# Linear attention's values as seven half-size products, with the norm's root moved behind the projections

## The chip, the cores and the metric

The kernel runs on one core of a Trainium2 chip. The metric is the device time of one execution in microseconds; the median of three runs of the kernel before is 2203.17 us (2202.41 to 2204.3). One more execution was taken by the hardware profiler, and all rows of the profile come from it.

## The reference

One layer of a hybrid encoder on 512 tokens of width 2048, in float32. What matters here is the first part:

```python
h = rms_norm(x, norm_mix_w[i])
proj = h @ w_in[i]
q_a, k_a, v_a, q_g, k_g, v_g, r_g, gate_lr = split_cols(proj, IN_SPLITS)
y_a = chunked_band_attention(q_a, k_a, v_a, att_rel_bias[i])          # 16 heads of 64
gate_logit = gate_lr @ w_gla_gate_up[i] + b_gla_gate[i]               # rank 16 -> 512
log_a = log_sigmoid(gate_logit) / GLA_GATE_TAU
o_g = gated_linear_attention(q_g, k_g, v_g, log_a)                    # 4 heads, values 256 wide
y_g = rms_norm(o_g, gla_norm_w[i]) * silu(r_g)
x = x + concat(y_a, y_g) @ w_out[i]
```

`rms_norm(x, w)` is `x * rsqrt(mean(x*x) + eps) * w`. Behind it come a gated MLP with a causal convolution (`w_ffn_up`, `w_ffn_down`), a gated per-layer embedding and a last norm; the change does not touch them.

## The kernel before, in words

**Products.** Every float32 operand is split into a rounded high half (`fp32r`, made by ScalarE with a copy) and a low half (the difference, made by VectorE), and a product of two is three matmuls: high by high, high by low, low by high. Most projections are done by Strassen's scheme in Winograd's form: a 2 x 2 block product with seven half-size products `P1` to `P7` instead of eight. Their operands are, on the weights' side, the four quarters `L11` to `L22` and the sums `S1` to `S4`, and on the input's side the quarters `R11`, `R21`, `R22` and the differences `N1`, `N2`, `T3`, `T4`. The results are collected into the quarters `C11`, `C12`, `C21`, `C22`.

**The front** has three parts, all on pages of 128 x 1024 weights (512 KB).
1. `first_values`: the first half of linear attention's values (`w_v_g`) as a plain product, eight pages (`values_page`, 24 matmuls of 512 columns each). Beside it `load_input` loads the sixteen tiles of x and splits each into the halves `h1`, weighted by `norm_mix_w`; `sq_acc` adds up the squares. At the last page `first_stats` makes the norm's root, by token (`rtok`) and spread over all partitions (`rb`), with the tiny matmuls `ms` and `pb`. `values_out` multiplies the values by `rtok`.
2. `second_values`: `gate_rank` first (`plr`, 32 matmuls on `h1`), then the other half of these values, eight pages again. Between pages VectorE and ScalarE scale x by weight and root (`scale_pair`), make the Strassen operands (`right`, `differences`, `spread_differences`) and run the forget gate (`gate_low`, `gate_up` with the matmuls `pz`, `gate_abs` to `gate_ln`). The list `todo` says at which page.
3. `values_product` for attention's values (`w_v_a`): seven products of four pages, 12 matmuls of 512 columns a page (tiles `vaA` to `vaD`). The sums `S1` to `S4` of weights are made by DMAs of the POOL queue that add in flight onto a page in SBUF (`sum_more`); two pages are summed on VectorE (`sum_right`). A page is split two pages ahead of its product (`value_split(v, n + 2)`); the dictionary `plan` says what else is done at which page.

TensorE, VectorE, ScalarE and in the third part also the SP and POOL queues follow the order in which the program writes these steps.

**After the front** the stage `in` makes, with seven products of 24 matmuls (256 columns) each, four units of keys and queries of linear attention (`linear`), eight of attention (`attend`) and four of the output gate (`after_gates`). Their input operands hold the norm's root already, so the results need no scaling. The work on a unit's result is put on an agenda, a list of (steps after the unit's end, place in the step, function). In `attend`, `low` makes the low halves of queries and, twice on different partitions, of keys (`Kl`). Then follow the output projection and the other stages, where the root `rb2` multiplies results of a projection (`after_up`, `after_gate`).

PSUM has eight banks: four for values (`psum_mm`) and four by turns for other things (`psum_aux`) in the front, and one pool of banks behind it.

Of the kernel before, what the change touches and what calls it, by code (L numbers as in the profile page):

```python
# [14 lines left out]
P = 128  # L15
T = 512
# [26 lines left out]
def encoder_block(ctx: ExitStack, tc: tile.TileContext, A, out):  # L43
# [8 lines left out]
    pctx = ExitStack()  # L52
    pm = pctx.enter_context(tc.tile_pool(name="pm", bufs=4, space=PSUM))
    pa = pctx.enter_context(tc.tile_pool(name="pa", bufs=4, space=PSUM))
# [31 lines left out]
    pw = pa.tile([P, T], F32, tag="aux", name="pw")  # L86
# [28 lines left out]
    aux = [lambda name: pa.tile([P, T], F32, tag="aux", name=name)]  # L115

    def psum_mm(name):
        return pm.tile([P, T], F32, tag="mm", name=name)

    def psum_aux(name):  # L120
        return aux[0](name)

    chores, hold = [], [1]
# [7 lines left out]
    def wtile(src, name, parts=1, between=None):  # L131
        n = src.shape[1]
        raw = page("wr", name + "_r")
        hi, lo = weight_pages()
        w = n // parts
        for i in range(parts):
            if i and between is not None:
                between()
            c = slice(i * w, (i + 1) * w)
            syn.dma_start(raw[:, c], src[:, c])  # L140
            act.activation(hi[:, c], raw[:, c], AF.Copy)
            vec.tensor_tensor(lo[:, c], raw[:, c], hi[:, c].bitcast(F32), ALU.subtract)
        for _ in range(hold[0]):
            if chores:
                chores.pop(0)()
        return hi, lo

    def mm3(po, whi, wlo, act, start, stop):
        nc.tensor.matmul(po, whi, act[:, 0, :], start=start, stop=False)
        nc.tensor.matmul(po, whi, act[:, 1, :], start=False, stop=False)  # L150
        nc.tensor.matmul(po, wlo, act[:, 0, :], start=False, stop=stop)

    def proj(po, srcs, acts, name, order=None):
        nk = len(acts)
        order = list(order or range(nk))
        per = 8
        tiles = {}
        for i, kt in enumerate(order):
            h = kt // per
            if h not in tiles:  # L160
                tiles[h] = srcs[h] if isinstance(srcs[h], tuple) else wtile(srcs[h], f"{name}_{h}")
            hi, lo = tiles[h]
            o = (kt % per) * P
            mm3(po, hi[:, o:o + P], lo[:, o:o + P], acts[kt], i == 0, i == nk - 1)

    def split(dst, src):
        nc.scalar.activation(dst[:, 0, :], src, AF.Copy)
        nc.vector.tensor_tensor(dst[:, 1, :], src, dst[:, 0, :].bitcast(F32), ALU.subtract)

    def split_scaled(dst, src, col):  # L170
        nc.scalar.activation(dst[:, 0, :], src, AF.Copy, scale=col)
        nc.vector.scalar_tensor_tensor(dst[:, 1, :], src, col, dst[:, 0, :].bitcast(F32), ALU.mult, ALU.subtract)

    def sq_acc(src, first, cl=slice(0, T)):
        if first:
            act.activation(acc[:, cl], src, AF.Square)
        else:
            s = tp.tile([P, T], F32, tag="sq", name="sq")[:, cl]
            act.activation(s, src, AF.Square)
            vec.tensor_tensor(acc[:, cl], acc[:, cl], s, ALU.add)  # L180

    def rstd_tok(parts, n, dst):
        nt = parts[0].shape[1] // P
        ms = psum_aux("ms")
        for t in range(nt):
            for i, sumsq in enumerate(parts):
                ten.matmul(ms[:, t:t + 1], sumsq[:, t * P:(t + 1) * P], ones[:, 0:1],
                                 start=i == 0, stop=i == len(parts) - 1)
        w = tp.tile([P, 4 * TT], F32, tag="tok", name="tok", bufs=2)
        a, y, t = w[:, 0:nt], w[:, TT:TT + nt], w[:, 2 * TT:2 * TT + nt]  # L190
        vec.tensor_scalar(a, ms[:, 0:nt], 1.0 / n, EPS, ALU.mult, ALU.add)
# [15 lines left out]
    def rstd_wide(ones_r, parts, n, dst, a):  # L207
        c = parts[0].shape[1]
        ms = psum_aux("msw")[:, :c]
        for i, q in enumerate(parts):  # L210
            ten.matmul(ms, ones_r, q, start=i == 0, stop=i == len(parts) - 1)
        act.activation(dst, ms, AF.Ln, scale=1.0 / n, bias=epst)
        t = tp.tile([P, T], F32, tag="dg", name="nwt")[:, :c]
        vec.tensor_scalar(a, ms, 1.0 / n, EPS, ALU.mult, ALU.add)
        act.activation(dst, dst, AF.Exp, scale=-0.5)
        vec.tensor_tensor(t, dst, dst, ALU.mult)
        vec.scalar_tensor_tensor(t, t, -0.5, a, ALU.mult, ALU.mult)
        vec.scalar_tensor_tensor(dst, t, 1.5, dst, ALU.add, ALU.mult)

    w_all = hp.tile([P, 6 * 1024 + 136], F32R, name="w")  # L220
    h_all = hp.tile([P, 8 * 2048], F32R, name="h1")

    def h_view(kt):
        return h_all[:, 1024 * kt:1024 * kt + 1024].rearrange("p (h t) -> p h t", h=2)
# [11 lines left out]
    h1 = []  # L236
    first = xslot(0, "x0_0")
    nc.scalar.dma_start(first, A["x"][0])
    nc.scalar.dma_start(cols, A["cols"])
    nc.scalar.activation(warm, ones[:, 0:1], AF.Copy)  # L240

    def load_input(kt):
        xt = xslot(kt, f"x0_{kt}") if kt else first
        if kt:
            nc.sync.dma_start(xt, A["x"][kt])
        h = h_view(kt)
        split_scaled(h, xt, nmix[:, kt:kt + 1])
        h1.append(h)
        return xt

    def first_values(src):
        ps = [psum_mm(f"v0_{t}") for t in range(TT)]
        for kp in range(KD // 2):
            if kp == 4:
                gate_weights()
            xs = []
            if kp > 0:
                xs.append(load_input(2 * kp))
            hi, lo = wtile(src[0, kp], f"wv0_{kp}", 2 if kp < 2 else 1,
                           (lambda: xs.append(load_input(0))) if kp == 0 else None)  # L260
            xs.append(load_input(2 * kp + 1))
            sq_acc(xs[0], kp == 0)
            sq_acc(xs[1], False)
            if kp == KD // 2 - 1:
                first_stats()
            values_page(ps, hi, lo, kp)
        values_out(ps, 0, [gt(f"t{t}") for t in range(TT)])

    def values_page(ps, hi, lo, kp):
        for j in range(2):  # L270
            kt = 2 * kp + j
            wh = hi[:, j * T:(j + 1) * T]
            wl = lo[:, j * T:(j + 1) * T]
            for t in range(TT):
                sl = slice(t * P, (t + 1) * P)
                ten.matmul(ps[t], h1[kt][:, 0, sl], wh, start=kt == 0, stop=False)
                ten.matmul(ps[t], h1[kt][:, 0, sl], wl, start=False, stop=False)
                ten.matmul(ps[t], h1[kt][:, 1, sl], wh, start=False, stop=kt == KD - 1)

    def values_out(ps, c, tiles, ts=range(TT)):  # L280
        for t in ts:
            act.activation(tiles[t], ps[t], AF.Copy, scale=rtok[:, t:t + 1])
            pool.dma_start(vgd[2 * c:2 * c + 2, :, t].rearrange("h p v -> p h v"),
                                tiles[t].rearrange("p (h v) -> p h v", h=2))

    def first_stats():
        rstd_tok([acc], D, rtok)
        nc.scalar.activation(rb, rstd_bc(rtok), AF.Copy)

# [46 lines left out]
    aux_tags = ["b4", "b5", "b6", "b7"]  # L336
# [437 lines left out]
    def attend(unit):  # L774
# [5 lines left out]

        def load_e():
            for s in range(2):
                nc.sync.dma_start(bias[0][:, s, :], A["bias"][2 * b + s])
# [85 lines left out]
        items = [(2, 7, load_e if b else lambda: None), (2, 2, high), (3, 1, low), (4, 1, mask), (5, 0, load_v), (11, 1, result)]  # L869
# [9 lines left out]
    def after_gates(unit):  # L879
# [14 lines left out]
        return [(0, 0, load), (0, 1, lambda: act.activation(unit.o, unit.o, AF.Silu)), (2 * (g in (1, 2)), 2, times), (2 * (g in (1, 2)), 3, pair)]  # L894
# [230 lines left out]
    VALUE_SLOTS = {"C11": 3, "C12": 3, "C22": 6, "C21": 7}  # L1125
    VALUE_ORDER = ("P1", "P2", "P4", "P5", "P6", "P3", "P7")
# [709 lines left out]
```

## Time and profile before

| | |
|---|---|
| median of three runs | 2203.17 us (2202.41 to 2204.3) |
| span of the profiled execution | 6266.3 us |
| TensorE busy in the span | 6253.6 us, 18248 matmuls |
| VectorE, ScalarE, GpSimd busy | 1910.0, 1349.7, 215.6 us |
| DMA | 561.39 MB in 200037 packets |
| first value matmul, last value matmul of the front | 10.1 us, about 637 us |

No other time of the profiled execution is given than its span, which is 2.84 times the median of the runs: the profile is of a much slower execution. Its rows say what was done, in which order and how long an operation took there; whether a wait shows in it depends on what else was slow. "Busy" is the time in which an engine works on at least one instruction; "DMA share" is the mean busy share of the 16 DMA engines. In the rows, `out<-in` are tiles by the program's names, followed by partitions x elements, the count, the busy time and the mean of one in ns, and then the idle time of the engine before them with what ended it.

### The profile page before, as it was taken

The page shows a single profiled execution, that of the slowest core. Times are in us where ns is not written, and L with a number is a line of the kernel's source. Part 1 is how long each engine was busy: PE and PEld are TensorE (multiplying, and loading weights), DVE is VectorE, ACT ScalarE, POOL GpSimd, SP SyncE. Part 2 cuts the span into 40 slices and gives each one's busy share as a digit, 9 for nine tenths or more (in the row PEclk, how much of TensorE's full clock was granted, in tenths as well). Part 3 has the DMA queues.
Part 4 walks back from the last instruction along what each step waited for, and adds up shares of the span by engine and source line. Part 5 has one row for each costly group of instructions (what it writes and reads, how often), then busy time and mean ns, then how long its engine had stood idle before and what let it go on. Part 6 is the DMA issues. An engine that isn't in the chain of part 4 may idle for free.

```text
span 6266.3 us, 45637 instructions
## 1 busy us (share of the span) xinstructions
PE 6253.6 (100%) x18248; PEld 5819.7 (93%) x18248; DVE 1910.0 (30%) x2585; ACT 1349.7 (22%) x1960; POOL 215.6 (3%) x261
## 2 busy tenths in 40 slices
PE   9999999999999999999999999999999999999999
PEld 5555999988989799999999999999999999999999
DVE  2222222222222233333333333333333232233333
ACT  2111111222221222222222222222222121222322
POOL 0000000000000000000000000000000000000000
DMA  1123222222222334344444443333333242333432
GB/s 67 34 81 64 61 71 57 72 74 63 70 70 87 110 100 122 101 108 116 113 113 103 112 107 92 83 78 87 79 108 95 61 113 70 109 101 114 121 110 88
DMA packets 200037, 561.39 MB, mean 90 GB/s; under 512 B 21808, under 2 KB 64048, under 8 KB 199824
## 3 DMA queue, kind: packets, MB, share of 16 engines
q1 hardware_dynamic: 163184, 431.28, 21.0%
q0 software_dynamic: 34656, 124.27, 11.5%
q8 instruction: 143, 2.34, 0.2%
q10 hardware_dynamic: 1984, 2.92, 0.1%
q14 instruction: 70, 0.57, 0.0%
HBM read 484.99 MB, written 119.54 MB: 96 GB/s over the span
## 4 chain that ended last, share of the span: by engine, by line
PE 100%; DVE 0%; issue 0%; DVEq 0%; ACT 0%; POOL 0%; POOLq 0%
PE accA L64 48%; PE accC L64 24%; PE accB L64 12%; PE v L64 5%; PE vaA L64 2%; PE vaC L64 1%; PE pp L64 1%; PE psc L64 1%; PE ptr L64 1%; PE py L64 1%; PE po L64 1%; PE vaD L64 1%; PE vaB L64 1%; PE plr L64 0%; PE pu L64 0%; PE pat L64 0%
## 5 line engine op out<-in xcount | busy, mean ns | idle before, releaser
L64 PE MATMUL accA<-h,w 128*128 128x256 f32 x5088 | 1695.5, 563 | 0.0
L64 PEld LDWEIGHTS accA<-h,w 128*128 128x128 f32 x5088 | 1673.7, 473 | 13.1 <-issue 11.6
L64 PE MATMUL accC<-h,w 128*128 128x256 f32 x4248 | 1347.7, 542 | 0.0
L64 PEld LDWEIGHTS accC<-h,w 128*128 128x128 f32 x4248 | 1330.8, 454 | 1.6 <-issue 0.6
L64 DVE TENSOR_TENSOR w<-s,w 128x1024 fp32r<-128x1024 f32 (+1 forms) x381 | 458.4, 1203 | 1100.4 <-ACT w L64 1100.4
L64 DVE TENSOR_TENSOR w<-l,w 128x1024 fp32r<-128x1024 f32 (+1 forms) x320 | 383.2, 1197 | 612.1 <-ACT w L64 607.6
L64 ACT ACTIVATE u<-accA 128x256 f32<-128x256 f32 x302 | 116.1, 384 | 2033.4 <-PE accA L64 2033.4
L64 ACT ACTIVATE w<-l 128x1024 fp32r<-128x1024 f32 (+1 forms) x320 | 331.8, 1037 | 956.1 <-PE accC L64 557.4
L64 ACT ACTIVATE w<-s 128x1024 fp32r<-128x1024 f32 (+1 forms) x381 | 395.0, 1037 | 327.5 <-PE accB L64 203.2
L64 PE MATMUL accA<-up_R,w 128*128 128x256 f32 x1056 | 325.3, 531 | 0.0
L64 PE MATMUL accA<-up_N,w 128*128 128x256 f32 x1056 | 324.2, 530 | 0.0
L64 PE MATMUL accB<-up_R,w 128*128 128x256 f32 x1056 | 323.7, 529 | 0.0
L64 PEld LDWEIGHTS accA<-up_R,w 128*128 128x128 f32 x1056 | 320.5, 441 | 1.6 <-issue 0.8
L64 PEld LDWEIGHTS accA<-up_N,w 128*128 128x128 f32 x1056 | 320.6, 442 | 0.0
L64 PEld LDWEIGHTS accB<-up_R,w 128*128 128x128 f32 x1056 | 320.5, 442 | 0.0
L64 PE MATMUL v<-w,h 128*128 128x512 f32 x384 | 318.6, 1100 | 0.0
L64 PEld LDWEIGHTS v<-w,h 128*128 128x128 f32 x384 | 165.2, 431 | 150.5 <-issue 150.1
L64 DVE TENSOR_TENSOR s<-s,l 128x1024 f32<-128x1024 f32 (+1 forms) x176 | 211.2, 1200 | 0.0
L64 DVE TENSOR_TENSOR u<-u,accC 128x256 f32<-128x256 f32 x102 | 43.0, 421 | 547.7 <-PE accC L64 547.7
L64 DVE TENSOR_TENSOR u<-u,accA 128x256 f32<-128x256 f32 x98 | 41.3, 421 | 510.4 <-PE accA L64 510.4
L64 DVE TENSOR_TENSOR u<-u,accB 128x256 f32<-128x256 f32 x100 | 42.1, 421 | 479.4 <-PE accB L64 479.4
L64 ACT ACTIVATE u<-accC 128x256 f32<-128x256 f32 x98 | 37.7, 384 | 603.5 <-PE accC L64 603.5
(303 smaller groups left out, 5554.9 us busy)
## 6 DMA issues: line engine op xcount, KB each, us to landing
l<-in_w_up SPq DMA_DIRECT2D x132, 512.0 KB, 3.5
s<-in_w_up SPq DMA_DIRECT2D x84, 512.0 KB, 3.5
s<-in_w_up POOLq DMA_DIRECT2D x84, 512.0 KB, 5.5
l<-in_w_dn SPq DMA_DIRECT2D x56, 448.0 KB, 3.4
l<-in_w_blk SPq DMA_DIRECT2D x48, 512.0 KB, 3.5
s<-in_w_blk SPq DMA_DIRECT2D x32, 512.0 KB, 3.5
s<-in_w_blk POOLq DMA_DIRECT2D x32, 512.0 KB, 6.1
l<-in_w_out SPq DMA_DIRECT2D x28, 512.0 KB, 3.6
```

Of the source, the lines that this page charges most:

```text
L64: ins = f(*args, **kw)
```

## The change

Linear attention's values are now made by seven half-size products too, and in turns with attention's. There is one list of steps, `VALUE_STEPS`: (g, P1), (a, P1), (g, P2), (a, P2), then P4, P5, P6, P3, P7 of `g` (linear attention) and of `a` (attention). Each has four pages, so 56 pages of 12 matmuls; `value_step(n)` loads, splits, does what `plan` has for page n, and multiplies.

- The products use operands without the norm's root: x times `norm_mix_w` alone (`split_weighted`, `weigh_left`, `differences`). The input halves `h1`, `scale_pair` and `sq_acc` are gone. x is loaded in halves of 256 tokens at first.
- The sum of squares comes from a second copy of x, by token (`xt`, eight pages of 512 KB): `token_load` at pages 16 to 23, `token_square` on ScalarE with an accumulated sum at pages 18 to 25, `token_norm` at page 26, with `pb`.
- The root then multiplies values by token on ScalarE (`value_scale`), the gate's low-rank product (as before), and the results of the `in` stage on VectorE by `rb2`: a `scale` step in `linear` and `attend`, and one ahead of SiLU in `after_gates`.
- `gate_rank` is at page 35 and works on Strassen operands: for the second half of the tokens it uses `R22` and `T3` with a second set of weights, `gls`, made by `gate_weights` at page 34. `gate_low` is at page 36, `gate_up` at 37 and 39.
- All `S` sums of `g` are made by DMAs that add in flight (16 pages); `a` keeps its 14 and two on VectorE.
- The banks are one pool from the start, with two (`b4`, `b5`) by turns for other things in the front.
- In `attend`, the second `Kl` is copied from the first by ScalarE (`low_copy`) instead of a second difference on VectorE.

```diff
+    VALUE_STEPS = [("g", "P1"), ("a", "P1"), ("g", "P2"), ("a", "P2")] + [(v, p) for v in "ga" for p in ("P4", "P5", "P6", "P3", "P7")]
+    VALUE_BANKS = {"gA": (0, 1), "aA": (2, 3), "gB": (4, 5), "aB": (6, 7), "gD": (4, 5), "gC": (6, 7), "aD": (6, 7), "aC": (0, 1)}
...
+    def value_step(n):
+        if n + 4 < len(vpages) and vpages[n + 4][1] in ("P1", "P2", "P4"):
+            value_load(*vpages[n + 4])
+        value_split(n + 2)
+        for f in plan.get(n, ()):
+            f()
...
+    def split_weighted(dst, c, src, kt):
+        col = nmix[:, kt:kt + 1]
+        act.activation(dst[:, 0, c], src, AF.Copy, scale=col)
+        vec.scalar_tensor_tensor(dst[:, 1, c], src, col, dst[:, 0, c].bitcast(F32), ALU.mult, ALU.subtract)
...
+    def token_square(i):
+        t = tokens.pop(i)
+        act.activation(t, t, AF.Square, accum_out=sums[:, i:i + 1])
+
+    def token_norm():
+        token_roots(rtok)
+        act.activation(rb, rstd_bc(rtok), AF.Copy)
...
+            (24, (collect_first, "g", "C22", "C", -1), (spread_differences, 6, "N2"), (spread_differences, 7, "N2"), (token_square, 6),
+             (sum_more, "g", "P3", 1, "L12"), (value_load, "g", "P7", 0)),
+            (25, (token_square, 7), (spread_differences, 0, "T3"), (spread_differences, 1, "T3"), (sum_more, "g", "P3", 2, "L12"),
+             (value_load, "g", "P7", 1)),
+            (26, (token_norm,), (right, 0, 1), (right, 1, 1), (sum_more, "g", "P3", 3, "L12"), (value_load, "g", "P7", 2),
+             (sum_more, "g", "P7", 0, "L11")),
...
+            (32, (collect_more, "g", "C12", "C"), (value_done, "g", "C12"), (sum_more, "a", "P5", 0, "L22")),
+            (33, (sum_load, "a", 2)), (34, (gate_weights,), (sum_more, "a", "P5", 1, "L22")),
+            (35, (gate_rank,), (sum_load, "a", 3)),
+            (36, (collect_more, "g", "C21", "A"), (collect_more, "g", "C22", "A"), (value_done, "g", "C21"), (value_done, "g", "C22"),
+             (gate_low,)),
+            (37, (gate_up, (0, 1)), (gate_abs, (0, 1)), (gate_min, (0, 1))), (38, (sum_right, "a", 2)),
...
-                for r in (a, z):
-                    vec.tensor_tensor(M["Kl", s][r], o[a, 1, :], M["Kh", s][a].bitcast(F32), ALU.subtract)
+                vec.tensor_tensor(M["Kl", s][a], o[a, 1, :], M["Kh", s][a].bitcast(F32), ALU.subtract)
+
+        def low_copy():
+            for s in range(2):
+                a, z = slice(s * 64, s * 64 + 64), slice(64 - s * 64, 128 - s * 64)
+                act.activation(M["Kl", s][z], M["Kl", s][a].bitcast(F32), AF.Copy)
...
-        return [(0, 0, load), (0, 1, lambda: act.activation(unit.o, unit.o, AF.Silu)), (2 * (g in (1, 2)), 2, times), (2 * (g in (1, 2)), 3, pair)]
+        return [(0, 0, load), (0, 1, lambda: vec.tensor_tensor(unit.o, unit.o, rb2, ALU.mult)),
+                (0, 2, lambda: act.activation(unit.o, unit.o, AF.Silu)), (2 * (g in (1, 2)), 2, times), (2 * (g in (1, 2)), 3, pair)]
```

More of the change, by code (lines that the diff above doesn't have):

```diff
@@ L234, in encoder_block @@
     gnw = cols[:, 4 * KD + 4:4 * KD + 6]
-    h1 = []
-    first = xslot(0, "x0_0")
-    nc.scalar.dma_start(first, A["x"][0])
+    first = xslot(0, "x0")
+    nc.scalar.dma_start(first[:, 0:256], A["x"][0][:, 0:256])
     nc.scalar.dma_start(cols, A["cols"])
     nc.scalar.activation(warm, ones[:, 0:1], AF.Copy)
[L242 to L288, printed above, removed]
     xa = []
@@ new lines, in left, with right @@
+    def left(k):
+        t, c = operand("R11", k // 4), slice(k % 4 * 256, k % 4 * 256 + 256)
+        split_weighted(t, c, xslot(k, "")[:, 0:256], k)
+        front.pieces["R11", k] = t[:, :, c]
+    def right(k, half):
+        t, o = operand(("R21", "N2")[k // 4], k // 2 % 2), k % 2 * 512
+        lo, hi = (0, 512) if half == 2 else (256 * half, 256 * half + 256)
+        split_weighted(t, slice(o + lo, o + hi), xslot(k + 8, "")[:, lo:hi], k + 8)
+        for i, name in enumerate(("R21", "R22")):
+            front.pieces[name, k] = t[:, :, o + 256 * i:o + 256 * i + 256]
@@ L1514, in linear_pages @@
         G["s"] = pg.tile([P, 2, T], F32R, tag="r6", name="squares")
-    va = dict(pages=[(p, j) for p in VALUE_ORDER for j in range(4)], raw={}, sum={}, l22={}, tiles={}, have=set())
     def at_page(n, *fs):
```

529 lines of the change are left out of this document (252 added, 277 removed).

## The prediction

> **What bounds the kernel now.** I first set the profiled execution beside the timed runs, for they do not agree (the clock by core, the page's first part, two pieces of the chain that ended last), then read the engines by stage in the windows, then the groups of instructions of the front, where the change lies, the DMA queues, and the timeline at the norm and the gates.
>
> ```profile
> core 0: 6266.3 us, clock 1.000
> span 6266.3 us, 45637 instructions
> PE 6253.6 (100%) x18248; PEld 5819.7 (93%) x18248; DVE 1910.0 (30%) x2585; ACT 1349.7 (22%) x1960; POOL 215.6 (3%) x261
> 401.40 39.38 PE vaB L64 x48
> 4577.40 14.36 PE accA L64 x48
> ```
>
> The profiled execution spans 6266.3 us; the median of the runs is 2203.17 us, 2.84 times less. TensorE is busy in all of the span, and nothing in the rows says why it is slow: the granted clock stands at 1.000. A 512-wide matmul of the front takes 39.38 / 48 = 0.82 us here, a 256-wide one of the later stages 14.36 / 48 = 0.30 us. In the runs the same 18248 matmuls, most of them 256 wide, fit into 2203.17 us, at most 0.121 us each, so at most 0.24 us for a 512-wide one. So TensorE runs about three times faster when timed. I know of nothing that would speed VectorE, ScalarE or the DMA engines alike, and take their durations over. Then 1910.0 us of VectorE is 87% of a timed run, not 30%, and waits that the profile hides behind slow matmuls are open in the runs. Sums below are for the runs' pace; the profile's own follows beside them.
>
> ```profile
> core 0: us, PE busy (x) PEld busy (x) DVE busy (x) ACT busy (x) POOL busy (x), PEclk, DMA share, GB/s
> 0.00:174.40 174.40, 173.20 (x224) 95.68 (x225) 32.67 (x52) 34.30 (x54) 5.00 (x17) 1.00 0.18 64
> 174.40:361.70 187.30, 187.30 (x229) 97.95 (x228) 45.42 (x69) 31.75 (x45) 0.73 (x1) 1.00 0.11 36
> 361.70:637.00 275.30, 275.30 (x337) 143.66 (x336) 60.78 (x75) 48.09 (x60) 20.78 (x25) 1.00 0.31 75
> 637.00:1150.00 513.00, 513.00 (x1231) 496.26 (x1231) 116.94 (x150) 82.84 (x111) 14.75 (x17) 1.00 0.25 66
> 1150.00:1900.00 750.00, 750.00 (x1934) 674.89 (x1934) 196.64 (x480) 164.76 (x316) 24.64 (x28) 1.00 0.26 69
> ```
>
> The first three rows are the front: the first half of linear attention's values, the gate's rank and the second half, then attention's values as seven products. Their 337 matmuls of the third row need at most 337 x 0.24 = 81 us in a run. There stand 60.8 us of VectorE, 48.1 of ScalarE and 0.31 x 275.3 = 85 us of DMA. So that part is near the limit of the DMA engines at the runs' pace, while the first two rows (0.18 x 174.4 = 31 us and 0.11 x 187.3 = 21 us, beside 224 and 229 matmuls) leave them half idle or more. In the attention row VectorE has 197 us against 1934 x 0.121 = 234 of TensorE.
>
> **The change, part by part.** *TensorE.* Both halves of linear attention's values are 384 matmuls, the others 336.
>
> ```profile
> L64 PE MATMUL v<-w,h 128*128 128x512 f32 x384 | 318.6, 1100 | 0.0
> L64 PE MATMUL plr<-h,g_S 128*128 128x512 f32 x32 | 26.6, 1093 | 0.0
> ```
>
> After, 14 products of 4 pages of 12 matmuls are 672, 48 fewer than 720. That is 48 x 0.82 = 39.4 us at the profile's pace, at most 48 x 0.24 = 11.5 us at the runs'; I take 11. The gate's rank becomes 64 matmuls of half the width, the same columns. The Trainium skill (TensorE: Matmul & The Clock Gate, "Wait — 56ns, not 53.3ns?") has a warm 512-wide matmul every 215.7 ns, by which the saving would be 10.4 us; the profile's 0.82 us does not agree with that, the bound from the runs does.
>
> *VectorE and ScalarE in the front.*
>
> ```profile
> L64 DVE TENSOR_TENSOR w<-wv_r,w 128x1024 fp32r<-128x1024 f32 x14 | 17.1, 1225 | 176.1 <-ACT w L64 176.1
> L64 DVE TENSOR_TENSOR acc<-acc,sq 128x512 f32<-128x512 f32 x15 | 10.3, 687 | 1.6 <-ACT sq L64 1.6
> L172 DVE SCALAR_TENSOR_TENSOR h<-pair_r,cols,h 128x512 fp32r<-128x512 f32 x10 | 7.4, 747 | 0.5 <-ACT h L171 0.5
> L64 DVE SCALAR_TENSOR_TENSOR pair_r<-pair_r,cols,rb 128x512 f32<-128x512 f32 x10 | 7.0, 745 | 0.0
> L64 ACT ACTIVATE w<-wv_r 128x1024 fp32r<-128x1024 f32 x14 | 14.7, 1056 | 156.7 <-PE v L64 109.4 <-issue 47.3
> L171 ACT ACTIVATE h<-pair_r,cols 128x512 fp32r<-128x512 f32 x10 | 7.0, 712 | 0.4 <-DMA cols<-in_cols 0.4
> L64 ACT ACTIVATE sq<-pair_r 128x512 f32<-128x512 f32 x9 | 5.6, 622 | 0.3
> L64 ACT ACTIVATE g_t<-v,rtok 128x512 f32<-128x512 f32 x6 | 4.0, 684 | 8.8 <-PE v L64 8.8
> ```
>
> VectorE loses 16 low halves of the input (0.747), 16 scalings by the root (0.745) and 15 additions of squares (0.687): 34.2 us. It gains 12 more page splits (1.225, 14.7 us), eight collects of about 0.69 (5.5), and some 4 us because operands are split in more, smaller pieces, with the gate's weights: net -10, from 139 to 129 us. ScalarE loses 16 high halves (0.712), 16 squares (0.622) and eight value outputs (0.684), 26.8 us; it gains 12 splits (12.7), eight squares of 1024 (8.5 by the split's row), eight weighings (5.7), eight collects and 16 scalings by the root (about 15), and some 5 us of smaller pieces: +20, from 114 to 134 us. TensorE has 672 + 32 matmuls, 169 us. On the whole both hide. But steps 0 to 11 (one step is a page, 12 matmuls, 2.9 us) hold 14 splits, the left operands, eight weighings, most right halves and four sets of differences: 31 us of ScalarE and 33 us of VectorE against 35 us of TensorE, each engine waiting on the other for every operand. With steps 16 to 22, where a product's pieces are split just ahead of it, I put 4 us of TensorE waits there (bounds 0 and 8).
>
> *DMA.* Page prices:
>
> ```profile
> q1 hardware_dynamic: 163184, 431.28, 21.0%
> q0 software_dynamic: 34656, 124.27, 11.5%
> wva_P_r<-in_w_v_a SPq DMA_DIRECT2D x16, 512.0 KB, 3.6
> wva_s<-in_w_v_a POOLq DMA_DIRECT2D x10, 512.0 KB, 5.7
> ```
>
> Queue 1 took 0.21 x 6266.3 us for 431.28 MB, 1.6 us for a 512 KB page; queue 0, mostly additions in flight, 0.115 x 6266.3 us for 124.27 MB, 3.0 us a page. The change makes 30 additions in flight of 14, four more page loads, and eight pages of x by token: 16 x 3.0 + 12 x 1.6 = 67 us more DMA in a front that is 11 us shorter. In steps 12 to 39 (28 steps and the rank, 89 us) stand 21 additions, some 29 loads and ten stores: 63 + 46 + 8 = 117 us by these prices, 21 x 1.6 + 46 + 8 = 88 us if an addition cost no more than a load. The pages are asked for three to four steps ahead of their split, some 10 us against 5.7 to land, so part of the excess is borrowed. I take 5 us of waits for late pages (0 and 12), nearer the low end, since the same density stands in the third window (85 of 81 us) for 28 steps already. The Trainium skill (Trainium Kernel Development and Optimization, "Key Constraints") has the DMAs of SP, ACT and POOL on the same 16 engines, interleaved; the prices here are shares of those 16 and agree, and were it otherwise these 5 us would be nought.
>
> *Three waits that get less cover.*
>
> ```profile
> 149.63 1.82 PE L64 MATMUL ms<-ones,acc 128*128 128x1 f32 x4
> 151.31 8.61 PE L64 MATMUL v<-w,h 128*128 128x512 f32 x10
> 159.76 3.52 PE L64 MATMUL pb<-dg,ones 128*128 128x512 f32 x2
> 151.49 0.16 DVE L64 TENSOR_SCALAR tok<-ms 128x4 f32<-128x4 f32 x1 [37.84 <-PE ms L64]
> 152.79 0.87 DVE L64 TENSOR_SCALAR dg<-ident,rtok 128x128 f32<-128x128 f32 x4
> 200.67 39.70 PE L64 MATMUL v<-w,h 128*128 128x512 f32 x48
> 240.20 3.52 PE L64 MATMUL pz<-g_t,g_t 128*128 128x512 f32 x4
> 201.02 0.68 DVE L64 TENSOR_TENSOR lf<-plr,rb 32x512 f32<-32x512 f32 x1 [17.24 <-PE plr L64]
> 201.73 1.28 ACT L64 ACTIVATE g_t<-lf 32x512 fp32r<-32x512 f32 x2 [19.21 <-DVE lf L64]
> ```
>
> The norm's chain on VectorE, 151.49 to 153.66, lies beside ten matmuls before `pb`. After, `token_norm` puts `pb` in front of step 26 with no matmul between: TensorE, in order, waits for the eighth token page, which rides behind the additions on three ring slots, its square, the split of page 28 and then those 2.2 us. I put 6 us (2, the bare chain, and 9). `gate_up` comes 48 matmuls after the rank now; after, 12 (2.9 us), while VectorE first splits a page and collects four accumulators (1.2 + 4 x 0.69), computes `lf`, and ScalarE makes four scalings and three copies: about 7.5 us, so 4.5 us of wait (2 and 6). The rank itself needs `gls`, in the page of a value quarter (C12) that must be collected, scaled and stored two steps before: 3 us (0 and 4). Behind the blocked `pb`, `plr` and `pz` every matmul of the step queues.
>
> *After the front.* The root multiplies 16 outputs of 1024.
>
> ```profile
> L64 DVE TENSOR_TENSOR u<-u,rb 128x1024 f32<-128x1024 f32 x50 | 61.2, 1223 | 147.8 <-ACT u L64 147.2 <-ACT rb L64 0.5
> L64 DVE TENSOR_TENSOR Kl<-u,Kh 64x512 fp32r<-64x512 f32 x32 | 22.0, 686 | 0.4
> L64 ACT ACTIVATE Kh<-u 64x512 fp32r<-64x512 f32 x28 | 17.4, 623 | 0.3
> ```
>
> VectorE gets 16 x 1.223 = 19.6 us: 4.9 in the linear units (117 us there against 149 of TensorE), 9.8 in attention, 4.9 at the output gates; attention gives back 16 of the 32 `Kl` differences, 11 us, to ScalarE as copies of 0.623, 10 us. Attention's VectorE is level, ScalarE goes to 175 of 234 us. The gates' SiLU starts one VectorE operation later. All of it is covered but for a collect now and then: 1 us (-3 and 6).
>
> **Sum.** -11 + 4 + 5 + 6 + 4.5 + 3 + 1 = +12.5 us; some 2 us that the old front must itself lose at its `ms` and late pages go with it: +10.5. All low ends (-11 + 2 + 2 - 3) give -10, and -12 with those 2; all high ends (-11 + 8 + 12 + 9 + 6 + 4 + 6) give +34. At the profile's pace a step is 12 x 0.82 = 9.8 us and covers all waits but the norm's: 6266.3 - 39.4 + 4 = 6231 us.
>
> **The rivals.** *TensorE stays the bound* (0.27). The splits run two pages ahead of their products, 5.8 us of lead that may swallow every wait but the bare chain of 2 us: 2203.2 - 11 + 2 = 2194 us. For it: TensorE is busy for 100% of the profile, and VectorE keeps 40 us of room in the front as a whole. Against: the 100% is at matmuls of 0.82 us. It decides once the front's new waits are under some 7 us. *The waits just eat the saving* (0.16): 2203 us, waits of 7 to 15 us. *DMA becomes the bound* (0.15): steps 12 to 39 take 117 us instead of 89, +28 - 11 + 10 for gate waits: 2230 us. For it: the third window's 85 us. Against: loads may slide ahead of step 12. The Trainium skill (TensorE: Matmul & The Clock Gate, "What's actually happening") halves the clock after an idle window of about 3.4 us; no row here can show it, and three such waits would add to this case.
>
> **How the numbers follow.** The forecast case, slower through the waits at `pb`, `pz`, `plr` and the crowded steps, has 0.42 and 2203.2 + 10.5 = 2213.7 us; its own range is 2208 to 2224. The case with the DMA bound lies above, so slower by over 0.2% (4.4 us, about what a measurement of this kernel can tell) has 0.57, within 0.16, faster 0.27. The range 2192 to 2229 leaves out the best of the first rival and half of the DMA rival.
>
> **What would show it.** A profile as slow as this one would show the 48 matmuls gone, a span near 6231 us and a longer run time none the less. Step by step: 672 value matmuls; idle PE before `pb` ended by VectorE `dg`; with faster matmuls also before `plr` and `pz`; a DMA share of 0.5 or more in the front's busy part; VectorE's front busy about 10 us less, ScalarE's 20 us more. The prediction is wrong if the run time falls by 8 us or more, or if the growth lies after the front, in attention.

## The result and the profile after

The changed kernel takes 2260.94 us (median of four runs, 2257.45 to 2263.76) against 2203.36 us for the kernel before, measured beside it: ratio 1.0257, interval 1.0243 to 1.0272. It is 57.6 us slower; the prediction had 10.5 us and a range up to 2229.

The profiled execution of before that the prediction reads was slow as a whole (6266.3 us; one of seven timed runs of the same kernel later was slow too, 5682.03 us), and since the profile after is at the runs' pace, before was profiled again for the comparison (`e0_before_again`). Its page, first part:

```profile
span 2203.6 us, 45637 instructions
PE 2180.6 (99%) x18248; PEld 2129.8 (97%) x18248; DVE 1873.8 (85%) x2585; ACT 1321.4 (60%) x1960; POOL 215.4 (10%) x261
```

The same of after:

```profile
span 2255.4 us, 45743 instructions
PE 2188.2 (97%) x18224; PEld 2134.9 (95%) x18224; DVE 1875.4 (83%) x2581; ACT 1351.0 (60%) x2018; POOL 227.1 (10%) x277
```

TensorE has 24 matmuls fewer (48 of 512 columns and the eight tiny `ms` are gone; 32 of the rank became 64 of half the width) and yet 7.6 us more busy time, and 67.2 us of the span without work instead of 23.0. Both mean waits: idle ones, and matmuls at a lower clock behind them.

To place them I cut both executions at the same four points: the first matmul of the `in` stage (the front's end), the first scores of attention, the first matmul of the square sums `pp`, the end. Windows of before:

```profile
core 0: us, PE busy (x) PEld busy (x) DVE busy (x) ACT busy (x) POOL busy (x), PEclk, DMA share, GB/s
0.00:184.50 184.50, 180.16 (x788) 148.20 (x789) 134.57 (x194) 112.75 (x159) 26.46 (x43) 0.99 0.70 203
184.50:333.50 149.00, 148.83 (x1282) 146.86 (x1281) 117.13 (x153) 82.48 (x112) 14.76 (x17) 1.00 0.84 230
333.50:584.20 250.70, 249.37 (x2243) 241.42 (x2241) 222.85 (x522) 175.68 (x344) 25.31 (x29) 1.00 0.89 252
584.20:2203.60 1619.40, 1602.21 (x13940) 1593.34 (x13940) 1399.21 (x1718) 950.53 (x1346) 148.85 (x172) 1.00 0.87 263
```

and of after, cut at the same matmuls:

```profile
0.00:213.10 213.10, 179.25 (x764) 145.33 (x765) 128.04 (x190) 129.68 (x197) 40.08 (x59) 0.91 0.89 245
213.10:376.10 163.00, 152.29 (x1282) 149.75 (x1281) 122.53 (x158) 89.02 (x122) 14.64 (x17) 0.97 0.79 217
376.10:635.60 259.50, 253.33 (x2242) 244.78 (x2241) 226.06 (x518) 181.94 (x354) 25.14 (x29) 0.99 0.87 244
635.60:2255.40 1619.80, 1603.29 (x13942) 1595.07 (x13940) 1398.76 (x1718) 950.38 (x1346) 147.25 (x172) 1.00 0.87 262
```

The front lost 28.6 us, linear attention's projections 14.0, attention with the output gates 8.8, the rest 0.4: the 51.8 us between the two spans. Each profile is one execution, after's the fastest of its four (2257.45 us) and before's a single one of 2205.31 us, so 51.8 and not 57.6 us are accounted for here. In the front the DMA engines went from 0.70 x 184.5 = 129 us to 0.89 x 213.1 = 190 us, and the granted clock (PEclk) fell from 0.99 to 0.91. TensorE's waits there, by what ended them (total, times, longest), before and then after:

```profile
PE vaA L64 <- ACT w L64: 1.3, 1, 1.3
PE v L64 <- ACT h L171: 1.1, 1, 1.1
PE vaA L64 <- DVE w L64: 0.8, 1, 0.8
```

```profile
PE pb L62 <- DVE dg L62: 9.0, 1, 9.0
PE plr L62 <- DVE g_S L62: 8.5, 1, 8.5
PE pz L62 <- ACT lr L62: 4.7, 1, 4.7
PE vgA L62 <- ACT in_R L62: 4.6, 2, 4.1
PE vgC L62 <- DVE g_t L62: 3.8, 1, 3.8
```

3.2 us before; 30.6 us in these five rows after. What stands behind three of the waits, and a fourth one behind the front, from after's timeline (start, length, engine, instruction, in brackets the idle time before it and its end):

```profile
93.66 1.06 ACT L62 ACTIVATE tokens<-tokens 128x1024 f32<-128x1024 f32 x1 [1.70 <-DMA tokens<-in_xt]
96.40 1.23 DVE L62 TENSOR_TENSOR w<-g_e,w 128x1024 fp32r<-128x1024 f32 x1 [0.49 <-ACT w L62]
98.97 0.88 DVE L62 TENSOR_SCALAR dg<-ident,rtok 128x128 f32<-128x128 f32 x4
99.90 2.08 PE L62 MATMUL pb<-dg,ones 128*128 128x512 f32 x2 [9.02 <-DVE dg L62]
...
134.50 0.28 ACT L62 ACTIVATE gls<-ident 128x96 fp32r<-128x96 f32 x1 [5.03 <-DMA vgd<-vgC]
135.60 5.37 PE L62 MATMUL plr<-in_R,g_S 128*128 128x256 f32 x24 [8.49 <-DVE g_S L62]
...
353.23 1.34 ACTq L1423 DMA_DIRECT2D ond<-g_e  x2
368.39 1.28 ACT L62 ACTIVATE Kh<-u 64x512 fp32r<-64x512 f32 x2 [10.38 <-DMA ond<-g_e]
370.80 1.22 PE L62 MATMUL accB<-in_R,w 128*128 128x256 f32 x4 [8.31 <-ACT w L62]
```

At `pb`, the last token page, its square, a split and the norm's chain stand one behind the other. `gls` lies in a page whose store to DRAM had to land first. And at 353 us linear attention's last outputs, now in tile `e1`, are stored from memory over which attention's `Kh` lies: ScalarE waits 10.38 us for the store, with a page split and TensorE behind it.

In the waits and behind them the clock is granted at half. Windows cut at these stretches:

```profile
11.00:17.83 6.83, 4.60 (x10) 3.21 (x11) 4.04 (x6) 3.72 (x6) 0.00 (x0) 0.50 0.96 328
72.40:75.80 3.40, 2.88 (x7) 2.30 (x8) 2.49 (x5) 1.58 (x3) 0.86 (x1) 0.50 1.00 258
92.90:103.14 10.24, 3.24 (x6) 1.92 (x7) 4.18 (x15) 5.32 (x10) 1.71 (x2) 0.50 1.06 276
130.50:140.74 10.24, 5.14 (x24) 5.14 (x25) 2.20 (x5) 2.15 (x5) 0.00 (x0) 0.50 1.05 314
154.40:161.20 6.80, 5.30 (x13) 4.14 (x14) 3.23 (x4) 3.62 (x6) 3.45 (x6) 0.50 0.71 189
366.00:376.24 10.24, 5.44 (x25) 5.44 (x26) 6.33 (x8) 6.76 (x10) 0.00 (x0) 0.50 0.25 75
601.50:604.90 3.40, 3.40 (x18) 3.40 (x18) 3.40 (x5) 0.93 (x3) 0.88 (x1) 0.50 0.78 239
sum 51.15, PE 30.00 PEld 25.55 DVE 25.86 ACT 24.08 POOL 6.89; mean PE 4.29 PEld 3.65 DVE 3.69 ACT 3.44 POOL 0.98
```

Seven stretches, 51.15 us, with 30.00 us of matmuls in them, which would take about half of that at full clock (a set of four 256-wide matmuls starts every 0.86 us in the stretch at 366 us, and every 0.45 us at 354 us): 15 us, 10.6 of them in the front.

### The profile page after: what moved, and what is told of

It is laid out like the page before. It is cut to its first block, busy times and chain, and to the rows that moved or that the text cites. A ratio compares the mean times of both kernels' runs of the same rounds, so it can differ in the third digit from the quotient of the medians.

```text
span 2255.4 us, 45743 instructions
## 1 busy us (share of the span) xinstructions
PE 2188.2 (97%) x18224; PEld 2134.9 (95%) x18224; DVE 1875.4 (83%) x2581; ACT 1351.0 (60%) x2018; POOL 227.1 (10%) x277
## 4 chain that ended last, share of the span: by engine, by line
PE 74%; DVE 8%; DMA 8%; ACT 5%; issue 3%; SPq 0%; POOL 0%; DVEq 0%; ACTq 0%; POOLq 0%
PE accA L62 38%; PE accC L62 19%; PE accB L62 10%; DVE w L62 3%; ACT w L62 2%; PE vaA L62 1%; DVE u L62 1%; DMA wvg_P_r<-in_w_v_g 1%; DVE h L62 1%; DMA s<-in_w_up 1%; PE py L62 1%; PE vgA L62 1%; DMA ond<-g_e 1%; DVE s L62 1%; PE psc L62 1%
## 5 line engine op out<-in xcount | busy, mean ns | idle before, releaser
L62 PE MATMUL accA<-h,w 128*128 128x256 f32 x5088 | 615.9, 278 | 5.4 <-ACT u L62 4.5
L62 PEld LDWEIGHTS accA<-h,w 128*128 128x128 f32 x5088 | 596.8, 188 | 8.7 <-ACT u L62 5.4
L62 PE MATMUL accC<-h,w 128*128 128x256 f32 x4248 | 510.5, 277 | 0.0
L62 PEld LDWEIGHTS accC<-h,w 128*128 128x128 f32 x4248 | 495.6, 188 | 0.3
L62 PE MATMUL accA<-up_R,w 128*128 128x256 f32 x1056 | 127.0, 276 | 0.0
L62 PE MATMUL accB<-up_R,w 128*128 128x256 f32 x1056 | 126.8, 276 | 0.0
L62 PE MATMUL accA<-up_N,w 128*128 128x256 f32 x1056 | 126.8, 276 | 0.1
L62 PEld LDWEIGHTS accA<-up_R,w 128*128 128x128 f32 x1056 | 123.0, 188 | 0.5 <-issue 0.5
L62 PEld LDWEIGHTS accA<-up_N,w 128*128 128x128 f32 x1056 | 122.9, 188 | 0.2 <-ACT u L62 0.2
L62 PEld LDWEIGHTS accB<-up_R,w 128*128 128x128 f32 x1056 | 123.1, 188 | 0.0
```

Source lines behind the costliest of these rows:

```text
L62: ins = f(*args, **kw)
```

## The experiments

All times are medians; each ratio is to the kernel before, measured beside the run. Differences from the changed kernel are between medians that were not measured side by side. By the ratios, each known to about 0.0015 (3 us), they come out up to 3 us otherwise, so a difference under some 4 us is not told from nothing. In the edits, long lines are shortened at the right and lines that only move other steps are left out.

**Before again.** 

> The kernel before, unchanged, for a profile at the pace of the timed runs (the first one spanned 6266.3 us). Both theories expect a span near 2201 us and the front's last value matmul near 180 us, with TensorE waits of at most 10 us in the front behind the first matmul; the changed kernel ends its front near 213 us and waits 34 us there. If before also waits over 25 us in its front, the waits named below are not the loss.

2205.31 us, its rows above; the front ended at 184.5 us, with no wait over 1.3 us.

**The root's spread later**: the matmul `pb` and `rb` at page 30 instead of 26.

```diff
+    def spread_root():
         act.activation(rb, rstd_bc(rtok), AF.Copy)
-            (30, (spread_differences, 4, "T3"),
+            (30, (spread_root,), (spread_differences, 4, "T3"),
```

> The changed kernel, with the spreading of the norm's root (the matmul pb and rb) moved from page 26 to page 30; the root by token stays at page 26. Theory A (the loss is the sum of single waits of TensorE for too short a lead): the 9.2 us before pb go, and the time falls by 8 to 10 us, to about 2252. Theory B (the front is full: DMA, VectorE and ScalarE set its pace, and a wait removed comes back at the next page): under 3 us fall, and the waits at pages 27 to 36 grow by the rest.

2257.6 us, ratio 1.0253 (1.0237 to 1.0269): 3.3 us less by the medians and 0.9 by the ratios, no gain that can be told: theory A missed. The wait only moved and shrank a little:

```profile
PE pb L62 <- DVE dg L62: 7.2, 1, 7.2
```

`dg` was made at page 30 too, in VectorE's queue behind the split of a late page.

**The gate's chain later**: `gate_rank` at page 37, `gate_low` at 38, `gate_up` at 41 and 43, the rest behind.

```diff
-            (35, (gate_rank,), (sum_load, "a", 3)),
+            (35, (sum_load, "a", 3)),
-             (gate_low,)),
+            (37, (gate_rank,)), (38, (gate_low,), (sum_right, "a", 2)),
-            (37, (gate_up, (0, 1)), (gate_abs, (0, 1)), (gate_min, (0, 1))), (38, (sum_right, "a", 2)),
+            (41, (gate_up, (0, 1)), (gate_abs, (0, 1)), (gate_min, (0, 1))),
```

> The changed kernel, with the gate's rank matmuls moved from page 35 to 37, gate_low to 38, gate_up to 41 and 43, and the rest of the gate three to four pages later. Theory A: the 8.65 us before plr and the 4.85 before pz go but for 1 to 2 us, the time falls by 11 to 13 us, to about 2249. Theory B: under 5 us fall.

2246.75 us, ratio 1.0205 (1.0188 to 1.0221): 14.2 us less (11.5 by the ratios): theory A. The wait at `pz` is gone from the list, that at `plr` is 2.4 us.

**Another tile** for the outputs of head 3:

```diff
-                o = gt(f"e{h // 2}", 1024)
+                o = gt(f"e{h // 2}" if h < 2 else "e3", 1024)
```

> The changed kernel, with the outputs of linear attention's last head in tile e3 instead of e1, so that attention's first tiles do not lie over a page whose store is still on its way. Theory A: the 8.5 us of TensorE wait at the first attention unit go, the time falls by 7 to 9 us, to about 2253. Theory B' (that wait is for something else, such as the weights that queue behind the front): the wait stays and the time is within 2 us of the changed kernel's 2261.

2248.55 us, ratio 1.0212 (1.0194 to 1.023): 12.4 us less (9.9 by the ratios), more than theory A. The 8.3 us ahead of `accB` are gone; with half of the 5.44 us of slow matmuls that stood behind them, 2.7, that makes 11.0.

**The three together**, with `dg` at page 27 and `pb` at 31.

```diff
+            (27, (root_diagonal,), (right, 2, 1), (right, 4, 1),
+            (31, (spread_root,), (sum_load, "a", 1)),
```

> The changed kernel with three moves at once: the root's spread over the partitions (`pb`, `rb`) goes to page 31 with its diagonal `dg` built on VectorE at page 27, the gate's chain starts at page 37 instead of 35 and its later steps follow, and head 3 of linear attention stores its gates' page through another tile (e3 for e1). Theory A (each wait of TensorE costs its own length and the half clock after it, and the waits are separate): the wait of 9.18 us ahead of `pb` goes with 10.2 us at half clock behind it, and the gate's moves bring what they brought alone; against the changed kernel -9 to -14 from `pb`, -13 to -15 from the gate, -11 to -13 from the tile, together -33 to -42, about 2222 us. Theory B (the waits only hand the time on: the late work of VectorE and of the transfers ends when it ends, and TensorE meets it one step on): the single gains do not add, no more than -24, about 2237 us or above.

2235.65 us, ratio 1.014 (1.0123 to 1.0156): 25.3 us less, nearer theory B (24 at most) than theory A (33 to 42). The gate's and the tile's parts alone give 26.6 (21.4 by the ratios), so the `pb` part added no more than these runs can tell, although the wait of 9.0 us itself is gone. What stands in the front now, partly as before and partly new:

```profile
PE vgC L62 <- DVE g_t L62: 3.8, 1, 3.8
PE vgA L62 <- DVE w L62: 3.0, 4, 0.8
PE vgA L62 <- ACT in_R L62: 2.7, 1, 2.7
PE plr L62 <- DVE g_S L62: 2.0, 1, 2.0
```

New is that four times a page of `vgA` is late by 0.8 us.

**Waits filled with products of no use**:

```diff
+    def fill(n):
+        t = psum_aux("fill")
+        for _ in range(n):
+            ten.matmul(t[:, :P], ones, ones, start=True, stop=True)
...
+            (26, (fill, 38), (token_norm,),
+            (35, (fill, 35), (gate_rank,), (sum_load, "a", 3)),
```

> The changed kernel with products of no use (128x128 by ones) on TensorE where it waits in the front: 14 ahead of page 1, 38 ahead of `pb`, 35 ahead of `plr`, 17 ahead of `pz`, each worth 0.213 us at full pace, together somewhat less than the four waits. The waits themselves stay, the idle time in them goes. Theory A (idle time of TensorE is what brings the half clock behind a wait): the periods at 0.5 behind 8.7, 90.5, 126.7 and 150.8 us go, which cost 3.4 + 5.1 + 5.1 + 3.4 = 17 us; the kernel comes out 13 to 17 us faster than the changed kernel, near 2246. Theory B (the granted clock follows something else, or the late work is late by itself and is met later on): less than 5 us, or slower by what of the fill sticks out, up to +4.

2251.45 us, ratio 1.0218 (1.0201 to 1.0234): 9.5 us less, between the theories. Windows of this run:

```profile
75.00:100.00 25.00, 24.01 (x143) 20.84 (x143) 16.14 (x31) 18.80 (x33) 5.95 (x7) 1.00 1.05 270
100.00:125.00 25.00, 25.00 (x115) 20.78 (x114) 12.49 (x17) 15.37 (x24) 8.18 (x11) 1.00 0.99 260
125.00:150.00 25.00, 24.00 (x187) 22.86 (x186) 8.71 (x13) 8.21 (x15) 3.49 (x5) 1.00 0.66 208
```

The clock is whole (it was 0.84 in 75 to 100 and 0.80 in 125 to 150), so TensorE's idleness is what halves it; the wait at `vgC`, which was not filled, keeps its slow stretch (0.93 in 50 to 75). The expectation was too large since it took half of each slow stretch; half of the matmul time in the four filled ones, (4.60 + 3.24 + 5.14 + 5.30) / 2 = 9.1 us, is near what came out (the front itself ends 6.9 us earlier, at 206.2).

**Small token pages**: 64 of 1024 columns loaded.

```diff
-        syn.dma_start(tokens[i], A["xt"][i])
+        syn.dma_start(tokens[i][:, 960:1024], A["xt"][i][:, 0:64])
...
-        act.activation(t, t, AF.Square, accum_out=sums[:, i:i + 1])
+        act.activation(t[:, 0:960].rearrange("p (a b) -> p a b", a=15), t[:, None, 960:1024].broadcast_to([P, 15, 64]),
+                       AF.Square, accum_out=sums[:, i:i + 1])
```

> The changed kernel with token pages of which only 64 of the 1024 columns are loaded; the squares are summed over 15 copies of these on ScalarE, so its work stays about the same. It leaves out 15/16 of x by token, so the root is another number. Theory A (the wait ahead of `pb` is set by the last token page, ready at 93.66 us because the queues between 70 and 95 us have more to move than they can): the wait of 9.18 us falls to 2 to 3 us and its half clock with it, -7 to -12 us against the changed kernel, 2249 to 2254. Theory B (ScalarE's or VectorE's own order sets it: the squares wait for their turn behind splits and collects): the wait stays above 6 us and the time within 4 us of the changed kernel.

2256.74 us, ratio 1.0234 (1.0215 to 1.0252): 4.2 us less, and the wait at `pb` is 5.3 us instead of 9.0: between the theories. So 3.7 us of it were the late page; 5.3 us are the queue of squares, splits and the norm's chain.

**The scalings behind the front alone**, in the kernel before.

```diff
+        items = [(2, 7, load_e if b else lambda: None), (1, 1, scale), (2, 2, high), (3, 1, low), (3, 2, low_copy), (4, 1, mask), (5, 0, load_v), (11, 1, result)]
...
+        return [(0, 0, load), (0, 1, lambda: vec.tensor_tensor(unit.o, unit.o, rb2, ALU.mult)),
...
+        return [(0, 0, load_v), (0, 1, scale), (1, 1, keys), (2, 1, queries), (2, 4, turn), (3, 1, mask), (3, 2, turned), (4, 1, from_start),
```

> The kernel before with only the part of the change behind the front: queries, keys and gates are multiplied by the spread root where they are used (linear attention, attention and the output gates, on VectorE), with the copy of the lower half of the keys on ScalarE. The root is then applied twice to these. Prediction's step: +1 (-3 to +6) against the kernel before, 2200 to 2209. Rival, from the profile of the changed kernel: the scalings of the output gates delay ScalarE's collects there (waits of 3.25 and 2.79 us), so +4 to +6 come from the gates alone, about 2208; the wait of the first attention unit's keys does not appear here, because there the page's store and load order is that of before.

2212.93 us, ratio 1.0041 (1.0028 to 1.0054): 10.3 us more (9.0 by the ratio), above the step's +6. Three parts of it were then run. The gates alone:

> The kernel before with the multiplication by the root at the four pairs of output gates alone (VectorE ahead of ScalarE's SiLU; the root is applied twice there). Theory A (ScalarE stands at the SiLU that waits for VectorE and its collects are late): half of what all scalings cost, +4 to +6 us, 2207 to 2209. Theory B (the gates hide it; attention is where it costs): within 2 us of before.

2206.21 us, ratio 1.0006 (0.9997 to 1.0016): theory B. The copies on ScalarE alone:

> The kernel before with one move in attention and nothing else: the lower halves of the keys for the other row group (16 of the 32 `Kl` differences on VectorE) come from ScalarE as copies behind VectorE's difference. Theory A (these copies stand in ScalarE's queue ahead of `PT`, for which TensorE waits ahead of `py`): +2 to +4 us, 2205 to 2207, and waits ahead of `py` of 1 us or more. Theory B (attention's cost is the multiplication by the root on VectorE): within 1.5 us of before, with no such waits.

2206.69 us, ratio 1.0005 (0.9994 to 1.0016): theory B in time, though waits of 0.8 us at `py` appear. Attention's multiplication and copies together:

> The kernel before with the attention part of the scalings alone: queries and keys are multiplied by the spread root on VectorE, and half of the `Kl` differences go to ScalarE as copies (the root is applied twice there). All scalings together cost 10.3 us, the gates alone 0.7 and the copies alone 1.2. Theory A (the multiplication on VectorE beside the copies on ScalarE is the cost: either engine alone had room, `PT` gets late when both are in the way): +5 to +8 us, 2208 to 2213. Theory B (each part has a little, and the cost comes only when linear attention, attention and gates are all later, each handing its delay on): no more than +3 us.

2212.11 us, ratio 1.0033 (1.002 to 1.0046): 7 to 8 us, theory A. TensorE's waits in attention there, where before has none at `py`:

```profile
PE py L64 <- ACT PT L64: 3.6, 3, 1.7
PE accA L64 <- ACT u L64: 1.1, 1, 1.1
```

Cut as above, attention with the gates takes 258.5 us here (333.0 to 591.5) against 250.7. The two rows are 4.7 of these 7.8 us; the remainder is in smaller gaps and stays open. Ahead of the wait of 1.7 us, ScalarE's queue has a pair of copies before `PT`:

```profile
352.92 1.28 ACT L64 ACTIVATE Kl<-Kl 64x512 fp32r<-64x512 f32 x2
355.19 0.85 ACT L64 ACTIVATE PT<-ptr 128x384 f32<-128x384 f32 x2
```

Attention's multiplication without the copies was not run, so that the cost needs both is not shown.

**Six moves**: the three, the collect of `a`'s `C11` at page 17 instead of 19, left operands earlier, SiLU a step later.

```diff
-            (19, (collect_first, "a", "C11", "A"), (collect_more, "a", "C11", "B"), (spread_differences, 2, "N1"),
+            (17, (collect_first, "a", "C11", "A"), (collect_more, "a", "C11", "B"), (differences, 7, first_half),
+    left(2)
+    left(3)
-                (0, 2, lambda: act.activation(unit.o, unit.o, AF.Silu)),
+                (1 * (g < 3), 2, lambda: act.activation(unit.o, unit.o, AF.Silu)),
```

> The kernel of the three moves with three more: the collect of the attention values' first quarter goes from page 19 to 17 (the wait of 3.92 us at 67.6 us was for VectorE's collect), left operands 2 and 3 are made ahead of the first page and the others a page earlier (the wait of 2.89 us at 8.7 us), and three of the four output gates' SiLU come a step later (the wait of 3.09 us at 573.7 us was for ScalarE's collect behind such a SiLU). Theory A (each wait with the half clock behind it): these are worth 2.9 + 1.7, 3.9 + 3.4 and 3.1 us with their clock, -12 to -15 us against the kernel of the three moves at 2235.65, so about 2222. Theory B (transfers limit the front, and TensorE only meets the late page somewhere else): the start and the collect give nothing, the gates 3 to 5 us, 2231 to 2236.

2230.94 us, ratio 1.0118 (1.0103 to 1.0133): against the three moves' 1.014 hardly better, theory B. No wait of the front was over 2.6 us, and yet it ended at 196.5 us (195.1 with three moves).

**Without the 16 new additions in flight**, on the three moves:

```diff
-        pool.dma_start(raw, value_page(v, name, j), accum_op=ALU.add)
+        if v == "a":
+            pool.dma_start(raw, value_page(v, name, j), accum_op=ALU.add)
```

> The kernel of the three moves without the 16 additions in flight of linear attention's values (they are new with the change; pages L21 alone stand in place of the sums, so these values are other numbers). Theory A (the DMA engines, whose share is 0.90 to 1.04 from 25 to 150 us there, limit the front): the share falls to 0.7 or less, the waits ahead of `vgA<-w` between 109 and 124 us (four of 1.03 us), of `vgC` and `plr` (2.17 us) go, and the time falls by 5 to 10 us, 2226 to 2231. Theory B (the order of work on VectorE and ScalarE makes these waits): the share falls, the waits stay, and the time is within 3 us of 2235.65.

2218.05 us, ratio 1.0057 (1.0041 to 1.0072): 17.6 us less than the three moves, more than theory A; the two profiled executions differ by 9.1 us (2229.4 and 2220.3), 10.1 of it in the front. The same window of the kernel with the three moves, and of this one:

```profile
25.00:125.00 100.00, 90.34 (x367) 69.27 (x366) 70.55 (x113) 68.40 (x108) 20.87 (x25) 0.97 0.97 275
```

```profile
25.00:125.00 100.00, 95.90 (x430) 78.51 (x429) 76.78 (x123) 71.39 (x116) 7.00 (x9) 0.98 0.70 229
```

With the DMA share at 0.70 instead of 0.97, 430 matmuls instead of 367 are done in these 100 us, and the front ends at 185.0 us. The four waits at `vgA` and that at `plr` are gone. The same edit in the changed kernel itself:

> The changed kernel itself, only without the 16 additions in flight of linear attention's values (pages L21 alone stand in place of the sums, so these values are other numbers). Theory A (the transfers, at a share of 0.91 to 1.03 between 25 and 125 us, make the late token page ahead of `pb` and the late `gls` ahead of `plr`): both waits, 9.18 and 8.65 us, fall below 4 us, and with the half clock behind them the time falls by 18 to 26 us against 2260.9, to 2235 to 2243. Theory B (the transfers cost only the small waits of about 1 us that the kernel of the three moves lost with them, and the big waits come from the order of work: the squares' turn on ScalarE and the collect, scaling and store ahead of `gls`): the waits stay above 6 us, the time falls by 6 to 12 us, 2249 to 2255.

2250.51 us, ratio 1.0207 (1.0191 to 1.0223): 10.4 us less, theory B's time; the waits lie between the theories:

```profile
PE pb L62 <- DVE dg L62: 5.9, 1, 5.9
PE plr L62 <- DVE g_S L62: 5.3, 1, 5.3
PE pz L62 <- ACT lr L62: 4.7, 1, 4.7
```

So some 3 us each at `pb` and `plr` are the transfers', 5 to 6 the order of work. And in the kernel of the six moves:

> The kernel of the six moves (the best try) without the 16 additions in flight (these values are other numbers). Its front then has neither the crowded transfers nor the waits that the moves are for. Theory A (what the six moves did not bring at 2230.9 was held by the transfers): the start, the collect and the gates give another 8 to 12 us against the kernel of the three moves without the additions, 2218.05, and the front ends at 176 to 180 us, below the 184.5 of the kernel before; 2206 to 2210. Theory B (VectorE and ScalarE hold them too): within 4 us of 2218.

2215.95 us, ratio 1.0058 (1.0044 to 1.0072): theory B, no better than the three moves without the additions. Its front ends at 182.0 us, where before's ends at 184.5 (181.5 to 182.3 in four of its variants): even without big waits and crowded transfers the front only draws level. TensorE is busy there for 174.6 us and idle for 7.4, in before's front of 181.6 us (with the scalings alone behind it) busy for 179.9 and idle for 1.7: about half of the saved 11 us is there, and small waits take it back.

No version that computes the reference beat the kernel before.

## Why the prediction was wrong

The sign and the three places in the front (`pb`, `plr`, `pz`) were right, the size was not: +57.6 instead of +10.5 us, and all the prediction's high ends together give only +34. What it took over from the slow profile held: VectorE's 1910.0 us are 1873.8 at the runs' pace, ScalarE's 1349.7 are 1321.4. By its own terms, with the rows shown:

- *48 matmuls, -11.* It stands: a group of 48 in before's front has 11.0 us of busy time.

```profile
L64 PE MATMUL vaA<-w,in_R 128*128 128x512 f32 x48 | 11.0, 389 | 0.0
```

- *Crowded steps, +4 (0 to 8).* The waits at `vgA` (operands) and `vgC` (a collect) are 8.4 us. Mis-sized; right in kind.
- *Late pages, +5 (0 to 12).* As waits for a page's split they hardly show (0.8 us or less each), but taking the 16 additions away brings 10.4 us in the changed kernel, and 9 to 18 where the other waits are moved. The extra DMA work was right (67 us predicted, 61 measured), the assumption that loads asked for 10 us ahead hide most of it was not.
- *`pb`, +6 (2 to 9).* 9.0 us, the upper end, by the chain named there; 3.7 of it the token page.
- *`pz`, +4.5 (2 to 6).* 4.7 us, by the chain named there.
- *`plr`, +3 (0 to 4).* 8.5 us: the first failed step. It named the collect, the scaling and the store of the page that `gls` lies in, but gave the landing of that store no time of its own; ScalarE waits 5.03 us for that alone, and without the additions in flight 3.2 of the 8.5 us go.
- *After the front, +1 (-3 to 6).* 23.2 us: the second failed step. 8.3 are the wait at `Kh` for a store from `e1`, which the prediction missed although the tile stands in the whole diff (`o = gt(f"e{h // 2}", 1024)`, where before had other tiles); 2.7 the clock behind it; most of the other 12.2 the scalings, which alone cost 9 to 10 us in the kernel before. "Attention's VectorE is level, ScalarE goes to 175 of 234 us" counted busy time; in part it is the order in ScalarE's queue, where the copies stand ahead of `PT` (waits of 3.6 us at `py`), and the remainder stays open.
- *The half clock.* The third failed step. It was named in a rival with no price and no place in the sum. It cost about 10.6 us in the front and 15 in all.

The front comes out by these: -11 + 30.6 + 2.1 (four smaller waits) + 10.6 less the 3.2 us of waits and 1.7 of slow clock that before has itself (one stretch of 3.4 us, at 151 us), 27.4 against 28.6 measured.

The DMA rival (2230 us) was right that the additions in flight cost time, but they are not the bound: steps 12 to 39 took 122 us, near its 117, yet they still take 116 us without the additions, at a DMA share of 0.57 instead of 0.86. That its length came out is luck. The first rival (2194, TensorE stays the bound) fell with the 100% of a slow profile: I wrote that this busyness belonged to matmuls of 0.82 us and still gave that case 0.27. The statement that a profile after would be slow again, near 6231 us, fell too.

The Trainium skill (TensorE: Matmul & The Clock Gate, "What's actually happening") gives the default half clock after an idle window of about 3.4 us and full clock after as long a busy one. This trace agrees on the states (1.00 and 0.50 alone) and the lengths (3.4, 6.8, 10.2 us); the filled waits show that busyness keeps the clock. It does not agree that only so long a wait does it: before's own stretch at 151 us follows waits of 1.3 and 0.8 us.

## What to carry to other kernels

Price a wait of TensorE near 3 us or longer with what follows it: here half of the matmul time in the next 3 to 10 us, 1 to 3 us a wait. When a buffer gets a new user, ask what must land before the next one may write it, with the store's own time: two of the largest errors were a store ahead of a page's reuse. And when matmuls are saved by adding DMA work and operand work beside them, compare each stage's DMA share and queue orders at the pace at which the kernel runs; the profile at a third of that pace hid these limits.

## What the hardware showed unexpectedly

The half clock does not follow from the length of one wait alone. In the kernel of the six moves and in the same kernel without the additions, `vgD` has the same two waits, 0.8 and 1.6 us, 3 us apart. From the timelines of the one and the other, the second wait:

```profile
65.86 1.67 PE L62 MATMUL vgD<-w,h 128*128 128x512 f32 x6 [1.59 <-ACT h L62]
```

```profile
65.22 2.93 PE L62 MATMUL vgD<-w,h 128*128 128x512 f32 x6 [1.61 <-ACT h L62]
```

Behind it six matmuls take 1.67 us in the first kernel and 2.93 in the second, whose clock then stands at 0.50; in 50 to 75 us the granted clock is 1.00 in the one and 0.86 in the other. What decides between the two is not shown by any run here.
